# A two-layer diffusion trunk on one core: the output projection split in two stages, scores over all 128 rows, and a searched order

## The chip, the core and the metric

The kernel runs on one core of a Trainium2 chip. A core has five engines that run side by side, each with its own list of instructions, in order: TensorE (PE) multiplies matrices and transposes, VectorE (DVE) and ScalarE (ACT) work on tiles element by element, GpSimd (POOL) does small side jobs, and SyncE (SP) issues transfers (DMA). They wait for each other through semaphores. The metric is the time of one execution on the device in microseconds (us).

## The reference

Two layers run over 256 latent tokens (a grid of 4 x 64) and 128 context tokens, width 1024. Cut to what matters:

```python
def layer(x, mod, lp):
    h = rms(x, g_mix) * (1 + mod[1]) + mod[0]
    cq, ckv, krope, na_q, na_k, na_v, df_q, df_k, df_v = split(h @ w_in)
    o_mla = softmax_attend(...)         # 6 heads of width 64, keys of 96
    o_na  = neighbourhood_attend(...)   # 6 heads of 64; latent keys get a learned bias or -1e30
    o_df  = diff_attend(...)            # 4 heads: softmax(s1) - lam * softmax(s2), then RMSNorm
    mix = concat([o_mla, o_na, o_df]) @ w_out         # 384 + 384 + 256 rows of w_out
    x = x + mod[2] * mix
    h = rms(x, g_ffn) * (1 + mod[4]) + mod[3]
    return x + mod[5] * ((silu(h @ w_gate) * (h @ w_up)) @ w_down)
```

Context tokens attend to context tokens; latent tokens attend to cached context keys and their latent keys in one softmax. The keys and values of the context are outputs too.

## The kernel before

**Layout.** All 384 tokens stand side by side in the columns; the residual `xT` is [128, 8, 384], eight blocks of 128 features. Each projection runs as three products (`mm3`, L321 to L323): weights and data are split into a high half in a reduced format and the rest (`wh`, `wl`, made by ACT at L254 and DVE at L260), and hi x hi, lo x hi and hi x lo are summed. Raw weights come by SP into a ring of three `raw` tiles; `wh` and `wl` are rings of three slots each.

**Stages of a layer.** The input projection (`g1`, products `wh,hh`) is cut into six column chunks. The latent heads ("MLA") need chunk 0, the differential heads chunks 1 and 2, the three pairs of neighbourhood heads chunks 3 to 5. Attention works in steps made by `soft`: a score product (`score`, L1037), the maximum of a row on DVE (`maxima`, L1045), the exponential on ACT with its row sum (`exps`, L1056), the division on DVE (`norm`, L1061 and L1066), a transpose on PE (`turn`, L1004), a copy by ACT, and then the product with the values (`out`, L1139 and L1142). `pair` does this for two heads of MLA (`mla`) or of the neighbourhood group (`near`); `diff` does it for one differential head. The result of a pair is one block of 128 rows for the output projection: blocks 0 to 2 (`oxh`, `oxl`) are MLA, 3 to 5 neighbourhood and 6 and 7 differential (`o`).

**Neighbourhood scores before.** The queries of two heads stand in one tile, one head in rows 0 to 63 and the other in rows 64 to 127, and so do the keys; a head's score product takes its 64 rows. For a latent query tile, `bias` (L1100) adds a [128, 256] bias to the latent part of the score in the accumulator, and then `maxima` reads all 384 columns.

**Output projection.** For each of eight output blocks m, eight row blocks k of `w_out` are summed in one accumulator (order `ks`); `gated` (L534) then adds the result, times its gate, to `xT`. Blocks 0 to 2 (`OUT_EARLY`) are tasks of the plan below, block 3 only gets its weights split in the plan (`AHEAD`), and blocks 3 to 7 follow after it. After each block come its square (`norm_square`, L456), the running sum (L464) and the gained, split rows `fh`, `fl` (`gain_split`, L528 and L529) for the feed-forward, whose gate and up projections follow (products `fh,wh`), then the down projection.

**What sets the order.** From a layer's start to output block 2, every piece of work is a `Task` with an engine, a duration in us, a priority, its predecessors and the buffers it takes (`take`) or frees (`ROOM`: three `z`, two `s`, two `t` accumulators, three `raw`, three `w`, ...). `Plan.order` runs a greedy simulation on these durations and on the hops between engines (`HOPS`): each free engine takes the ready task of lowest priority number whose buffers are free. The instructions are then emitted in order of the tasks' planned starts, and each engine keeps that order. Dense work (`DENSE`) has high numbers and fills in. The durations are the planner's, not the chip's. Behind the plan, a scheduler of the compiler orders the engines' work.

## Time and profile before

| | |
|---|---|
| median of 3 runs (lowest to highest) | 1035.77 us (1035.76 to 1036.49) |
| profiled execution | 1036.13 us, span 1034.4 us |
| granted PE clock, mean | 0.986 |
| PE busy | 1012.3 us, 98%, 6074 matmuls |
| DVE, ACT, POOL busy | 719.5, 509.1 and 172.7 us |
| read from memory | 158.12 MB |

The span runs from the first to the last instruction. An engine is busy while one of its instructions runs. Matmuls overlap in the pipeline, so the time from one start to the next is what a matmul costs in a row of them, and a row's duration is longer. A type of f32 is written for both formats in PE's rows, and one product in full format shows as two matmuls. Layer 0 attends until about 215 us, layer 1 from about 545 to 717.

### The profile page before, as it was taken

The numbers are of one execution on the slowest core, as the hardware profiler recorded it, in microseconds if no ns is written. First come the engines' busy times: TensorE is split into PE (matmuls) and PEld (weight loads), VectorE is DVE, ScalarE is ACT, GpSimd is POOL, SyncE is SP. The second block draws the span as 40 slices with busy tenths as digits, with TensorE's granted clock in tenths as the row PEclk, the third lists the DMA queues.
The fourth block names the chain that finished last, engine by engine and source line by source line (L and its number), as shares of the span: only waits on it lengthen the run. The fifth ranks groups of instructions, "written<-read, shape, count | busy, mean of one in ns | idle before, by whom it ended". The sixth has DMA issues, their size and how long they took to land.

```text
span 1034.4 us, 16528 instructions
## 1 busy us (share of the span) xinstructions
PE 1012.3 (98%) x6074; PEld 933.0 (90%) x6074; DVE 719.5 (70%) x1599; ACT 509.1 (49%) x1180; POOL 172.7 (17%) x263
## 2 busy tenths in 40 slices
PE   8999999989999999999999999989999999999998
PEld 7877779679999999999978878867999999999998
DVE  5677787955999999963455887766869755554332
ACT  3466778745433333343326668766653334333221
POOL 2266223201001001100024533230010000000000
PEclk9999999989999999999999999969999999999999
DMA  9865444125575757684463232410376434343441
GB/s 356 331 202 190 161 153 138 58 82 202 165 243 185 233 177 232 206 273 131 123 226 101 81 125 71 154 54 9 123 249 199 125 120 137 108 123 111 139 137 42
DMA packets 129681, 162.25 MB, mean 157 GB/s; under 512 B 5056, under 2 KB 111680, under 8 KB 127296
## 3 DMA queue, kind: packets, MB, share of 16 engines
q1 hardware_dynamic: 121184, 132.76, 40.3%
q0 software_dynamic: 6832, 27.77, 7.7%
q8 instruction: 48, 0.79, 0.3%
q10 hardware_dynamic: 1584, 0.66, 0.2%
q14 instruction: 33, 0.27, 0.1%
HBM read 158.12 MB, written 3.05 MB: 156 GB/s over the span
## 4 chain that ended last, share of the span: by engine, by line
PE 76%; DVE 2%; ACT 1%; POOL 1%; issue 1%; ACTq 0%; DVEq 0%; POOLq 0%
PE z L321 11%; PE z L323 11%; PE z L322 11%; PE t L322 6%; PE t L321 6%; PE t L323 6%; PE s L322 5%; PE s L323 5%; PE s L321 5%; PE s L1037 2%; PE t L1004 2%; PE t L1139 1%; POOL small L542 1%; PE t L1376 1%; PE z L1037 1%
## 5 line engine op out<-in xcount | busy, mean ns | idle before, releaser
L254 ACT ACTIVATE wh<-raw 128x1024 fp32r<-128x1024 f32 (+2 forms) x216 | 201.5, 934 | 366.0 <-PE z L322 138.8
L260 DVE TENSOR_TENSOR wl<-raw,wh 128x1024 fp32r<-128x1024 f32 (+2 forms) x216 | 230.7, 1070 | 111.6 <-ACT wh L254 111.2
L321 PE MATMUL z<-fh,wh 128*128 128x386 f32 x304 | 103.2, 339 | 0.0
L322 PE MATMUL z<-fl,wh 128*128 128x386 f32 x304 | 103.0, 339 | 0.0
L323 PE MATMUL z<-fh,wl 128*128 128x386 f32 x304 | 102.6, 338 | 0.0
L444 DVE CUSTOM_DVE_ANT_0 sums<-wt,sums,pcol 128x1024 f32<-128x1024 f32 x80 | 102.2, 1278 | 0.3 <-DVE small L1578 0.3
L321 PE MATMUL z<-wh,hh 128*128 128x384 f32 (+1 forms) x264 | 99.9, 379 | 1.1 <-ACT hh L514 0.5
L323 PE MATMUL z<-wh,hl 128*128 128x384 f32 (+1 forms) x264 | 90.3, 342 | 0.5 <-DVE hl L522 0.5
L322 PE MATMUL z<-wl,hh 128*128 128x384 f32 (+1 forms) x264 | 89.8, 340 | 0.0
L542 POOL TENSOR_TENSOR small<-small,mhalf 128x4 f32<-128x4 f32 (+4 forms) x58 | 73.2, 1262 | 4.8
L321 PE MATMUL s<-fh,wh 128*128 128x386 f32 x200 | 68.2, 341 | 0.0
L321 PE MATMUL t<-fh,wh 128*128 128x386 f32 x200 | 68.1, 340 | 0.0
L322 PE MATMUL t<-fl,wh 128*128 128x386 f32 x200 | 67.8, 339 | 0.0
L322 PE MATMUL s<-fl,wh 128*128 128x386 f32 x200 | 67.8, 339 | 0.0
L323 PE MATMUL t<-fh,wl 128*128 128x386 f32 x200 | 67.5, 338 | 0.0
L323 PE MATMUL s<-fh,wl 128*128 128x386 f32 x200 | 67.5, 338 | 0.0
L438 POOL DMA_DIRECT2D wt<-in_w_modT x40 | 21.5, 539 | 273.7 <-DVE mod L444 190.8
L321 PEld LDWEIGHTS z<-wh,hh 128*128 128x128 f32 x264 | 49.8, 189 | 9.2 <-issue 4.2
L322 PEld LDWEIGHTS z<-fl,wh 128*128 128x128 f32 x304 | 57.5, 189 | 0.0
L323 PEld LDWEIGHTS z<-fh,wl 128*128 128x128 f32 x304 | 57.3, 188 | 0.0
L321 PEld LDWEIGHTS z<-fh,wh 128*128 128x128 f32 x304 | 57.2, 188 | 0.0
L1056 ACT ACTIVATE e<-s,small 128x384 f32<-128x384 f32 (+1 forms) x102 | 51.0, 506 | 12.2 <-DVE small L1045 11.2
(316 smaller groups left out, 2422.8 us busy)
## 6 DMA issues: line engine op xcount, KB each, us to landing
raw<-in_w_gate SPq DMA_DIRECT2D x22, 1024.0 KB, 6.0
raw<-in_w_up SPq DMA_DIRECT2D x22, 1024.0 KB, 5.4
raw<-in_w_down SPq DMA_DIRECT2D x32, 704.0 KB, 4.8
wt<-in_w_modT POOLq DMA_DIRECT2D x40, 512.0 KB, 4.3
raw<-in_w_mod SPq DMA_DIRECT2D x16, 1024.0 KB, 5.0
raw<-in_w_in SPq DMA_DIRECT2D x40, 384.0 KB, 3.9
raw<-in_w_out SPq DMA_DIRECT2D x8, 1024.0 KB, 5.5
qu<-in_w_mod SPq DMA_DIRECT2D x8, 512.0 KB, 7.4
```

The costliest lines, as they stand in the source:

```text
L254: nc.scalar.activation(hi, src, AF.Copy)
L260: nc.vector.tensor_tensor(lo, src, hi.bitcast(F32), op=ALU.subtract)
L321: nc.tensor.matmul(out, sh, mh, start=first, stop=False)
L322: nc.tensor.matmul(out, sh, ml, start=False, stop=False)
L323: nc.tensor.matmul(out, sl, mh, start=False, stop=last)
L438: nc.gpsimd.dma_start(self.w[:, self.loaded % 3], w_modT[l, c * P:(c + 1) * P])
L444: nc.vector.tensor_tensor_reduce(self.junk, self.w[:, self.n % 3], self.s[:, v], 1.0, pcol[l][:, PC_BMOD + c:PC_BMOD + c + 1], ALU.mult, A ...
L542: nc.gpsimd.tensor_tensor(out, t[:, :n], mhalf[:, :n], op=ALU.pow)
L1004: nc.tensor.transpose(pt[:, b, :], x, ident)
L1037: nc.tensor.matmul(ps[:, i, :], q, k, start=True, stop=True)
L1056: nc.scalar.activation(x["e"][i], ps[:, j, :], AF.Exp, bias=x["mx"][:, i:i + 1], accum_out=x["su"][:, i:i + 1])
L1139: nc.tensor.matmul(po[64 * i:64 * i + 64, 0:NL], vv[:, b, v0 + i, :], p["pT"][i][:, b, :], start=(b == 0), stop=(b == 2), tile_position=(0 ...
```

## The change

1. *Two stages.* The first three row blocks of the output projection (the MLA heads) become tasks of their own for all eight output blocks: three `mm3` into a `z` accumulator, and a `gated` that adds them to `xT` at once (`part`). Their weights come in two transfers of [3, 512] and four splits of [3, 256]. The second stage sums the other five row blocks; its weights are [5, 256] a transfer and [5, 128] a split, and it adds to `xT` with a second `gated`.

2. *Full-row scores.* Each neighbourhood head gets a query tile of 128 rows with zeros in the other head's half; `naq` becomes a two-column scale with a zero half in each column, and ACT writes the queries twice. The tiles are four (`nu[0]`), used in turn by six heads, so the transposes of the last pair wait for the scores of the first (`na_last`). The keys stay shared. The bias table is [128, 5, 128] with zeros for the context keys, and one `tensor_tensor_reduce` adds it, negates, writes the row back and takes the negated maximum; `exps` then scales by -1. The context scores of two heads share one accumulator.

3. *Order.* Some durations and hops of the planner change. `Plan.best` runs `order` up to 300 more times, each time with the priorities of 1 to 40 drawn tasks changed, and keeps the plan with the earliest planned end.

```diff
-HOPS = {('pe', 'act'): 0.2, ('pe', 'dve'): 0.16, ('act', 'pe'): 0.22, ('dve', 'pe'): 0.27, ('pool', 'dve'): 0.06, ('act', 'dve'): 0.15, ('dve', 'act'): 0.15}
+HOPS = {('pe', 'act'): 0.22, ('pe', 'dve'): 0.22, ('act', 'pe'): 0.22, ('dve', 'pe'): 0.27, ('pool', 'dve'): 0.18, ('dve', 'pool'): 0.18, ('act', 'dve'): 0.15, ('dve', 'act'): 0.13}
...
+    def best(self):
...
+        for _ in range(ORDERS):
+            p = list(best)
+            for i in draw.sample(free, draw.choice((1, 2, 4, 8, 16, 40))):
+                p[i] = base[i] + draw.gauss(0, STIR if draw.random() < 0.8 else 5 * STIR)
+            try:
+                run(p)
+            except AssertionError:
+                continue
+            if self.end <= end:
+                end, best = self.end, p
+        return run(best)
...
+            for q in range(4):
+                w_order.append((("lat", l, q), ("lat", l, q // 2), w_out[l, 0:3 * P, q // 2 * 512:(q // 2 + 1) * 512].rearrange("(k p) c -> p k c", p=P), [3, 512],
+                                slice(0, 3), slice(q % 2 * 256, (q % 2 + 1) * 256), (3, 256)))
...
             def maxima():
+                x["mx"], i = small(n), 0
                 if bias:
-                    bias(x["b"][0][0])
-                x["mx"], i = small(n), 0
+
+                    s = x["b"][0][0][:, 0, :]
+                    s = s.rearrange("p (b k) -> p b k", k=P)
+                    nc.vector.tensor_tensor_reduce(s, s, bias(), -1.0, 3e38, ALU.add, ALU.min, x["mx"])
+                    return
...
-                    nc.scalar.activation(nu[0][:, j, t * P:(t + 1) * P], x["pt"][:, 0], AF.Copy, scale=naq)
+                    for i in range(2):
+                        nc.scalar.activation(nu[0][(2 * j + i) % 4][:, t * P:(t + 1) * P], x["pt"][:, 0], AF.Copy, scale=naq[:, i:i + 1])
...
-        ks = [0, 1, 2, 6, 7, 3, 4, 5]
+        ks = [6, 7, 3, 4, 5]
...
+        for q in range(4):
+            hi, lo, w, lead = weights(("lat", l, q), lead if q % 2 else None)
+            for m in (2 * q, 2 * q + 1):
+                x, prev = {}, None
+                for k in range(3):
...
+                        mm3(x["po"][:, :NT], w["h"][:, k, ms], w["l"][:, k, ms], *o_hl[k], k == 0, k == 2)
+                    prev = add(PE, 0.53, unit, after=[lo, prev, o_ready[k]], take=("z",) if k == 0 else (), frees=[hi], prio=DENSE + 1)
...
+                part.append(add(DVE, 0.82, lambda m=m, x=x: gated(l, m, x["po"], 16), after=[prev, gates], frees=[room], prio=DENSE / 2))
...
-        work = plan.order()
+        work = plan.best()
```

**Where rows move.** A row names line, operation, output <- inputs (with buffer numbers) and shape. First PE near the end of attention in layer 1. Before, from the transposes of the last neighbourhood pair (`tok`) on:

```order
L1209 MATMUL t_7823<-ident,tok_7736 128x128 x2
L1037 MATMUL z_7835<-ku_7112,qu_7111 128x384
L1004 MATMUL t_7843<-ident,e_7789 128x128 x3
L1209 MATMUL t_7859<-ident,tok_7763 128x128 x2
L1037 MATMUL z_7862<-ku_7112,qu_7111 128x384
L1376 MATMUL t_7870<-vd_6337,pd_7864 128x64 x3
L1004 MATMUL t_7880<-ident,e_7818 128x128 x3
L1004 MATMUL t_7893<-ident,dn_7288 128x128 x3
L1335 MATMUL t_7904<-identr,tok_7838 128x128 x4
L1376 MATMUL z_7930<-vd_6337,pd_7891 128x64 x3
L1335 MATMUL t_7942<-identr,tok_7847 128x128 x4
L1335 MATMUL t_7947<-identr,tok_7900 128x128 x4
```

Now, the stretch ahead of the last value product (`z_8314` and `z_8348` collect the latent row blocks, `dn` is a differential head):

```order
L1045 MATMUL t_8298<-ident,e_8259 128x128 x3
L1045 MATMUL t_8305<-ident,e_8266 128x128 x3
L357 MATMUL z_8314<-oxh_5911,wh_8058 128x384
L358 MATMUL z_8314<-oxl_5912,wh_8058 128x384
L359 MATMUL z_8314<-oxh_5911,wl_8078 128x384
L1045 MATMUL t_8322<-ident,e_8286 128x128 x3
L357 MATMUL z_8314<-oxh_5911,wh_8058 128x384
L358 MATMUL z_8314<-oxl_5912,wh_8058 128x384
L359 MATMUL z_8314<-oxh_5911,wl_8078 128x384
L1045 MATMUL t_8335<-ident,e_8295 128x128 x3
L357 MATMUL z_8314<-oxh_5911,wh_8058 128x384
```

Before, 37 rows in a line there (from the first score of that kind in a `z` accumulator to the first `oxh` row) belong to no projection; now transposes and latent row blocks take turns, and 54 of the layer's 72 latent row-block products come before the last value product.

Second, DVE in layer 0 just after the last neighbourhood pair. Before, from the first residual update (`xT`) on:

```order
L534 SCALAR_TENSOR_TENSOR xT<-z_2741,mod_101,xT 128x256
L534 SCALAR_TENSOR_TENSOR xT<-z_2741,mod_101,xT 128x128
L534 SCALAR_TENSOR_TENSOR xT<-z_2791,mod_101,xT 128x256
L534 SCALAR_TENSOR_TENSOR xT<-z_2791,mod_101,xT 128x128
L534 SCALAR_TENSOR_TENSOR xT<-z_2986,mod_101,xT 128x256
L534 SCALAR_TENSOR_TENSOR xT<-z_2986,mod_101,xT 128x128
L529 SCALAR_TENSOR_TENSOR fl_3058<-xT,aff_103,fh_3057 128x256
L529 SCALAR_TENSOR_TENSOR fl_3058<-xT,aff_103,fh_3057 128x128
L529 SCALAR_TENSOR_TENSOR fl_3058<-xT,aff_103,fh_3057 128x256
L464 TENSOR_TENSOR sq_3039<-sq_3039,sq_3043 128x384
L260 TENSOR_TENSOR wl_3048<-raw_2342,wh_3030 128x1024
L260 TENSOR_TENSOR wl_3076<-raw_3072,wh_3074 128x1024
```

Now, from the remainder of that pair's output (`o`) on:

```order
L1196 TENSOR_TENSOR o_2775<-t_3035,o_2774 128x384
L1619 TENSOR_TENSOR fl_3141<-mod_101,fh_3140 128x8x2
L570 SCALAR_TENSOR_TENSOR xT<-z_3050,mod_101,xT 128x256
L570 SCALAR_TENSOR_TENSOR xT<-z_3050,mod_101,xT 128x128
L291 TENSOR_TENSOR wl_3079<-raw_2686,wh_3072 128x640
L565 SCALAR_TENSOR_TENSOR fl_3141<-xT,aff_103,fh_3140 128x256
L570 SCALAR_TENSOR_TENSOR xT<-z_3068,mod_101,xT 128x256
L570 SCALAR_TENSOR_TENSOR xT<-z_3068,mod_101,xT 128x128
L565 SCALAR_TENSOR_TENSOR fl_3141<-xT,aff_103,fh_3140 128x128
L291 TENSOR_TENSOR wl_3098<-raw_2861,wh_3090 128x640
L570 SCALAR_TENSOR_TENSOR xT<-z_3094,mod_101,xT 128x256
L570 SCALAR_TENSOR_TENSOR xT<-z_3094,mod_101,xT 128x128
```

Before, three blocks' updates stand in a line ahead of the next splits (`wl`); now an update and a split of 640 columns take turns.

Third, SP in layer 0. Before:

```order
L1092 DMA bias_2042<-in_bias 128x384
L1092 DMA bias_2102<-in_bias 128x384
L244 DMA raw_2134<-in_w_out 128x8x256
L1190 DMA vn_2188<-in_cache 128x256
L1302 DMA tok_2279<-in_dfk 32x256 x4
L244 DMA raw_2342<-in_w_out 128x8x256
L244 DMA raw_3072<-in_w_out 128x8x256
L1204 DMA out_newc<-brief_2350 128x128
L244 DMA raw_3116<-in_w_out 128x8x256
L1204 DMA out_newc<-brief_2644 128x128
L1092 DMA bias_2774<-in_bias 128x384
L1092 DMA bias_2833<-in_bias 128x384
```

Now:

```order
L1137 DMA bias_2229<-in_bias 128x640
L1236 DMA vn_2278<-in_cache 128x256
L275 DMA raw_2292<-in_w_out 128x3x512
L1250 DMA out_newc<-brief_2454 128x128
L275 DMA raw_2500<-in_w_out 128x3x512
L1137 DMA bias_2547<-in_bias 128x640
L1137 DMA bias_2601<-in_bias 128x640
L275 DMA raw_2686<-in_w_out 128x5x256
L1250 DMA out_newc<-brief_2825 128x128
L275 DMA raw_2861<-in_w_out 128x5x256
L275 DMA raw_3155<-in_w_out 128x5x256
L275 DMA raw_3190<-in_w_out 128x5x256
```

The loads of `w_out` were four in a layer and are six, the first two for the latent rows; the last two bias tables moved from behind the last `w_out` load to ahead of the third.

## The prediction

> **What bounds the kernel now.** The page comes first: who is busy, and the clock by slices.

> ```profile
> span 1034.4 us, 16528 instructions
> ...
> PE 1012.3 (98%) x6074; PEld 933.0 (90%) x6074; DVE 719.5 (70%) x1599; ACT 509.1 (49%) x1180; POOL 172.7 (17%) x263
> ...
> PEclk9999999989999999999999999969999999999999
> ```

> TensorE (PE) is busy 98% of the span, so only PE's time counts. Two of the forty clock digits are below 9: the ninth slice and, far lower, the 27th. Next come busy times by stretch; "x" counts instructions, PEclk is the granted clock.

> ```profile
> core 0: us, PE busy (x) PEld busy (x) DVE busy (x) ACT busy (x) POOL busy (x), PEclk, DMA share, GB/s
> ...
> 50.00:215.00 165.00, 162.19 (x1034) 127.13 (x1034) 127.24 (x357) 120.91 (x384) 61.06 (x90) 1.00 0.45 144
> 215.00:230.00 15.00, 11.33 (x50) 10.12 (x49) 9.36 (x21) 6.92 (x13) 0.00 (x0) 0.77 0.38 120
> 230.00:525.00 295.00, 295.00 (x1680) 293.65 (x1679) 229.85 (x427) 114.13 (x173) 21.17 (x39) 1.00 0.61 197
> ...
> 545.00:675.00 130.00, 126.16 (x749) 109.33 (x750) 99.81 (x262) 93.83 (x285) 52.80 (x76) 1.00 0.33 105
> 675.00:700.00 25.00, 22.38 (x87) 14.31 (x87) 16.77 (x48) 15.34 (x54) 9.08 (x16) 0.59 0.17 53
> 700.00:725.00 25.00, 24.52 (x156) 19.24 (x155) 17.01 (x50) 16.31 (x53) 1.11 (x2) 1.00 0.01 1
> ```

> From 230 to 525 (layer 0's last output blocks and its feed-forward) PE never idles at full clock: 1680 matmuls in 295 us, 0.176 us each, and nothing to win. What a stretch loses is its idle time (length less busy) and its clock loss (length times 1 - PEclk):
> - 215:230, the output projection of layer 0: 3.67 idle + 0.23 x 15 = 3.45, so 7.1 us.
> - 675:700, the end of attention in layer 1: 2.62 + 0.41 x 25 = 10.25, so 12.9 us.
> - 50:215, 545:675 and 700:725: idle 2.81, 3.84 and 0.48, so 7.1 us.

> PE's timeline shows why. Columns: start, duration, engine, line, names, rows x columns, moving shape, count, idle before. First layer 1:

> ```profile
> 673.99 0.34 PE L323 MATMUL z<-wh,hl 128*128 128x384 f32 x1
> ...
> 677.07 0.76 PE L1037 MATMUL s<-ku,qu 64*128 64x128 f32 x4
> 678.62 0.66 PE L1209 MATMUL t<-ident,tok 128*128 128x128 f32 x2 [0.79 <-ACT e L1056]
> 679.21 1.65 PE L1037 MATMUL z<-ku,qu 64*128 64x384 f32 x2
> ...
> 690.03 1.95 PE L1335 MATMUL t<-identr,tok 128*128 128x128 f32 x8
> ```

> The last input projection ran at 673.99; after it only links of the softmax chains are left. The same score pair that takes 0.91 us warm (656.04 below) takes 1.65 at 679.21: half clock. The idle before 678.62 is only 0.79 us, so thin work alone cooled it. Now layer 0:

> ```profile
> 217.78 0.44 PE L321 MATMUL z<-oxh,wh 128*128 128x384 f32 x1
> ...
> 218.73 0.45 PE L321 MATMUL s<-oxh,wh 128*128 128x384 f32 x1 [0.32 <-ACT wh L254]
> ...
> 220.08 0.45 PE L321 MATMUL z<-oxh,wh 128*128 128x384 f32 x1 [0.72 <-ACT wh L254]
> 220.36 0.34 PE L322 MATMUL z<-oxl,wh 128*128 128x384 f32 x1
> 223.32 0.69 PE L323 MATMUL z<-oxh,wl 128*128 128x384 f32 x1 [2.62 <-DVE wl L260]
> ```
> ```profile
> 216.85 2.04 DVE L534 SCALAR_TENSOR_TENSOR xT<-z,mod,xT 128x256 f32<-128x256 f32 x6 [1.66 <-PE z L323]
> ...
> 222.05 3.49 DVE L260 TENSOR_TENSOR wl<-raw,wh 128x1024 fp32r<-128x1024 f32 x3
> ...
> 229.47 0.74 DVE L534 SCALAR_TENSOR_TENSOR xT<-z,mod,xT 128x256 f32<-128x256 f32 x2 [2.54 <-PE z L323]
> 230.44 1.23 DVE L260 TENSOR_TENSOR wl<-raw,wh 128x1024 fp32r<-128x1024 f32 x1 [0.22 <-ACT wh L254]
> 231.58 0.74 DVE L529 SCALAR_TENSOR_TENSOR fl<-xT,aff,fh 128x256 fp32r<-128x256 f32 x2
> 232.24 0.55 DVE L464 TENSOR_TENSOR sq<-sq,sq 128x384 f32<-128x384 f32 x1
> ```

> PE waits 0.32, 0.72 and 2.62 us for weight halves of the later output blocks. The three early blocks end together, since each holds one of three weight slots until its last row block arrives; the next weights are split only then, and on VectorE (DVE) behind six residual updates (2.04 us). The gap costs the clock too (0.77 above).

> **The change part by part.**

> (a) *Full-row scores.* In the neighbourhood group, 24 score products (3 pairs, 2 heads, 2 query tiles, 2 layers) go from 64 rows to 128, with zeros in the other head's half. Scores of this type have 64 or 96 rows in the trace; each first row below is followed by PE's next work.

> ```profile
> 108.92 0.81 PE L1037 MATMUL s<-ku,qu 96*128 96x384 f32 x2
> 109.57 0.49 PE L1004 MATMUL t<-ident,e 128*128 128x128 f32 x3
> ```
> ```profile
> 656.04 0.91 PE L1037 MATMUL s<-ku,qu 64*128 64x384 f32 x2
> 656.88 0.44 PE L1209 MATMUL t<-ident,tok 128*128 128x128 f32 x2
> ```
> ```profile
> 147.02 1.55 PE L1037 MATMUL s<-ku,qu 64*128 64x384 f32 x4
> 148.51 0.45 PE L321 MATMUL z<-wh,hh 128*128 128x384 f32 x1
> ```

> 96 rows take 0.65 us from start to next start, 64 rows 0.84. I take 0.65 for 128 rows, being no half of the array: 20 warm scores x -0.19 = -3.8 us (four lie in the cold stretch, counted in (b)). Ends: two 64-row scores of different halves side by side took 1.49 together, 0.745 each, so 24 x -0.095 = -2.3; the other end 24 x -0.19 = -4.6. [...]

> (b) *End of attention, layer 1.* The eight output blocks' first three row blocks (72 matmuls a layer) now need only latent heads, and input projection is spread further: in the new order its last 12 matmuls stand beside the last pair's transposes, and 54 of the 72 follow before the last value product; before, 37 rows there held no projection at all. 54 x 0.176 = 9.5 us of dense work, moved, not added. If it keeps the clock, up to 12.9 us go. The last pair's chain (four scores, maxima, exponentials, transposes) stays and waits somewhere: I keep 1.5 us. A latent block also holds one of three z banks until its residual update; a late one stops PE's next block and all behind it, which rival 4 prices. Take -11.4; ends 0 and -12.9.

> (c) *Output projection, layer 0.* After the last value product the blocks run one after another, 15 matmuls (2.63 us) each, and slots come free one by one, so a split has two blocks' time. Take -6.6 of 7.1; ends 0 and -7.1. Late next is (e).

> (d) *The other stalls, 7.1 us.* The searched order changes everywhere, from a planner whose durations are raised towards the measured. Some stalls go, others come: half, -3.5; ends +3.5 and -7.1.

> (e) *VectorE in the output stage.* Residual update 0.74, second half of the gained rows 0.74, sum 0.55 (rows above) and the split of 640 columns:

> ```profile
> L444 DVE CUSTOM_DVE_ANT_0 sums<-wt,sums,pcol 128x1024 f32<-128x1024 f32 x80 | 102.2, 1278 | 0.3 <-DVE small L1578 0.3
> ...
> L1045 DVE TENSOR_REDUCE small<-s 128x1 f32<-128x384 f32 x67 | 35.7, 552 | 4.6 <-PE s L1037 3.7
> L260 DVE TENSOR_TENSOR wl<-raw,wh 128x640 fp32r<-128x640 f32 x32 | 26.4, 825 | 52.0 <-ACT wh L254 52.0
> ...
> L1100 DVE TENSOR_TENSOR s<-s,bias 128x256 f32<-128x256 f32 x17 | 7.2, 426 | 1.4 <-PE s L1037 1.2
> ...
> L444 DVE DVE_READ_ACCUMULATOR2_ANT mod<- 128x1 f32 x80 | 6.6, 82 | 0.0
> ```

> That is 2.86 us per block against PE's 2.63; before it was 3.26 against 24 x 0.176 = 4.2. Five blocks a layer: 5 x 0.23 = 1.2 us late at the feed-forward, twice: +2 (ends 0 and +5, if the two gate splits of 1.23 queue as well).

> (f) *VectorE and ScalarE in attention.* Sixteen more residual updates: 16 x 0.74 = +11.8 us. Bias add (0.426) and maximum (0.552) of 24 scores, 23.5 us, become one custom operation reading PSUM, which the trace does not show at 384 columns. By the 1024-column one of 1.278 scaled, 0.48 + 0.08 read-out; unscaled, 1.36. I take 0.65, nearest the maximum over the same 384: 15.6. Net +4 us on VectorE, beside PE while the windows below hold; 0 on the path, up to +13 at 1.36 (rival 4).

> ```profile
> 175.00:200.00 25.00, 23.81 (x150) 18.79 (x149) 22.35 (x64) 20.15 (x66) 7.01 (x11) 1.00 0.21 64
> ```
> ```profile
> L1212 ACT ACTIVATE qu<-t,naq 128x128 f32<-128x128 f32 x17 | 6.0, 367 | 3.8 <-PE t L1209 2.8 <-ACT vn L1193 0.4 <-DVE ku L1215 0.4
> ```

> Queries are written twice: 18 x 0.367 = 6.6 us more on ScalarE, which has 4.85 of 25 us free there even in the fullest stretch: 0.

> (g) *Queues.* SP issues six w_out loads a layer instead of four, same bytes, and larger bias tables (320 KB for 192). The last two bias tables now wait in SP's queue for a table to come free, ahead of the third w_out load of layer 0 and the fourth of layer 1; the gate weights stand behind those.

> ```profile
> DMA to landing us min/median/max: 2.2/3.1/10.3
> ```

> At a median 3.1 us (5.2 scaled by size) and tens of us ahead, 0; ends 0 and +2. POOL gains nothing.

> (h) *Added wait.* Six heads share four query buffers, so the last pair's transposes on PE wait for the first pair's scores; the order has both pairs' scores well ahead. Behind them stand projection rows: 0, at most the last link of (b).

> Sum: -3.8 - 11.4 - 6.6 - 3.5 + 2 = -23.3 us. The profiled execution took 1036.13 us (span 1034.4 and 1.7 around it), 0.4 above the median of 1035.77; 1036.1 - 23.3 = 1012.8.

> **The rivals.**

> 1. *Layer 1 stays cold.* The 54 products may be too thin between transposes. For it: the clock fell behind an idle of 0.79 us. Against: before there was no projection row at all. (b) gives 0 and (d) 2.5: 1036.1 - 3.8 - 6.6 - 2.5 + 2 = 1025.2. [...]

> 2. *Every stall goes.* -3.8 - 12.9 - 7.1 - 7.1 = -30.9, so 1005.2. For it: idle that moves behind filler vanishes. Against: the last chain, and (e).

> 3. *The order does nothing on the chip.* The search minimizes its own plan, whose durations are no trace; stalls would return elsewhere, about 1035. Against: (a) and (c) hang on no fine timing.

> 4. *Slower: the custom operation binds VectorE.* Place: neighbourhood scores, 175 to 215 and 650 to 700. VectorE has 2.65 of 25 us free, 4.2 in 40, 8.5 in two layers; its extra is 11.8 + 24 (x - 0.978). From x = 0.83 us it overflows. At 1.36 it is 21 us, 12.5 beyond the room: PE waits for maxima, (a), (b) and (d) fall away, 1036.1 - 6.6 + 12.5 + 2 = 1044. Slower than before from an overflow of 4.6 us, x = 1.03. For it: the only such row is 1.278; against: it has 1024 columns.

> **How the numbers follow.** My forecast (1006 to 1020) 0.62; rival 1 0.18; rival 2 0.08; rival 3 0.05; rival 4 0.07. Predicted: 1012.8. The range 1003 to 1027 takes in the forecast and rivals 1 and 2 with a margin for gaps the windows count as busy; it leaves out rivals 3 and 4, 0.12. A measurement tells 0.2% (2.1 us) from no change. Faster 0.62 + 0.18 + 0.08 and 0.01 of rival 3 = 0.89; same 0.03; slower 0.07 + 0.01 = 0.08.

> **What would show it.** (a): 128-row scores with 0.65 us to the next start. (b): clock 1.00 in every 25 us stretch of layer 1. (c): no wait above 1 us for weight halves after the last value product of layer 0. (d): idle outside these stretches near 3.5 us. (e): PE idle or repeated waits for fh, fl where the feed-forward begins, 1 us a layer. (f): the custom operation near 0.65 us. It is wrong if one clock digit stays near 6 in layer 1's attention, if VectorE passes 23 of 25 us there, or if the start to 50 us, which I leave as it is, grows.

## The result and the profile after

The changed kernel took 1010.96 us (median of 4 runs, 1010.33 to 1011.29) beside 1036.13 of the kernel before on the same chip: ratio 0.9753, 95% interval 0.9736 to 0.977, 25.2 us faster. The prediction was 1012.8, within 1003 to 1027. The profiled execution took 1011.29. One execution further down, the profiled one of experiment 6 (1649 us), ran at a granted clock of 0.555 over its whole span and serves no comparison. The page of the changed kernel, span, busy times and clock by slices:

```profile
span 1009.5 us, 16623 instructions
...
PE 995.5 (99%) x6074; PEld 929.6 (92%) x6074; DVE 721.8 (71%) x1637; ACT 512.6 (51%) x1206; POOL 174.4 (17%) x263
...
PEclk9999999999999999999999999999999999999999
```

No digit of the clock below 9 is left. The same stretches as before (columns as there; they are fixed in time, and from layer 0's feed-forward on the changed kernel's work stands 10 us or more earlier in them):

```profile
50.00:215.00 165.00, 162.18 (x1051) 131.06 (x1044) 129.94 (x370) 122.73 (x391) 61.59 (x90) 1.00 0.45 145
215.00:230.00 15.00, 15.00 (x87) 15.00 (x87) 12.98 (x31) 10.33 (x21) 0.00 (x0) 1.00 0.60 185
230.00:525.00 295.00, 294.01 (x1688) 289.14 (x1690) 228.93 (x431) 112.92 (x169) 24.08 (x42) 1.00 0.63 202
525.00:545.00 20.00, 18.00 (x84) 14.87 (x77) 13.11 (x29) 9.73 (x30) 11.16 (x18) 0.91 0.34 125
545.00:675.00 130.00, 129.01 (x798) 112.02 (x797) 105.68 (x288) 100.99 (x320) 56.09 (x79) 1.00 0.33 105
675.00:700.00 25.00, 23.63 (x155) 19.66 (x155) 22.29 (x67) 19.50 (x61) 5.37 (x7) 1.00 0.21 64
700.00:725.00 25.00, 25.00 (x146) 24.81 (x143) 20.99 (x47) 15.33 (x32) 0.00 (x0) 1.00 0.49 154
```

The output stage of layer 0 (215:230) has neither idle time nor clock loss, where 7.1 us stood. The end of attention in layer 1 (675:700) lost 12.9 us and now loses 1.37, all of it idle. Idle in 545:675 fell from 3.84 to 0.99; in 50:215 it did not move (2.81, now 2.82). Between 230 and 545 more is lost than before: idle 2.99 us against 1.65, in part because work that stood after 545 has moved in, and one piece of 3.41 us at half clock at 536.0. Before, the last of these stretches was:

```profile
525.00:545.00 20.00, 18.35 (x113) 13.17 (x111) 12.58 (x25) 6.65 (x11) 9.60 (x14) 1.00 0.69 228
```

The attention of layer 1, which before goes on to 723.1, now ends at 700.1. PE's timeline of 676 to 680 shows what stands there:

```profile
676.51 0.60 PE L1078 MATMUL s<-ku,qu 128*128 128x384 f32 x2
676.95 0.34 PE L357 MATMUL z<-oxh,wh 128*128 128x384 f32 x1
...
678.36 0.34 PE L359 MATMUL z<-oxh,wl 128*128 128x384 f32 x1
679.28 0.41 PE L1255 MATMUL t<-ident,tok 128*128 128x128 f32 x2 [0.58 <-DVE tok L1270]
679.44 0.42 PE L357 MATMUL z<-oxh,wh 128*128 128x384 f32 x1
```

Latent row blocks (`oxh,wh`) stand on both sides of the wait for `tok`, where before only transposes and scores stood. At the start, the first input product moved back from 21.05 to 22.87 us, behind products of the modulation, one of which waits for a transfer. Up to there PE has done 128 matmuls of the modulation instead of 96 and was idle for 2.13 us instead of 2.40, so the delay is work done earlier and not a loss:

```profile
21.87 0.30 PE L408 MATMUL m<-ku,sv 128*32 128x128 f32 x2 [0.87 <-DMA ku<-in_w_mod]
...
22.87 0.46 PE L357 MATMUL z<-wh,hh 128*128 128x416 f32 x1
```

The custom operation in the trace's list of one line's instructions (shortest, median and longest ns):

```profile
L1087 DVE DVE_READ_ACCUMULATOR2_ANT small<- x24: 83/141/144, 138.5 to 692.1; 128x1 f32 x24
...
L1087 DVE CUSTOM_DVE_ANT_0 s<-s,bias x11: 555/566/600, 139.6 to 690.5; 128x384 f32<-128x384 f32 x11
```

0.57 us and 0.14 for reading the accumulator out: 0.70 where 0.65 was taken.

Two tables compare all kernels. Both are worked out from one profiled execution each; those of S and R ran above their medians (1036.9 and 1034.9 us). In the first, idle is the span less PE's busy time, clock loss is half of the time that the trace's clock record holds at half clock (the piece at the very end of a span left out), and the rest is busy time less clock loss, in us (an estimate: not all work took twice as long at half clock, as the score row of 679.21 in the prediction, 1.65 us beside 0.91 at 656.04):

| kernel | median | against before | span | idle | clock loss | rest |
|---|---|---|---|---|---|---|
| before | 1036.1 | | 1034.4 | 22.1 | 13.7 | 998.7 |
| S: two stages | 1033.0 | -3.5 | 1035.1 | 19.6 | 17.1 | 998.4 |
| R: full-row scores | 1032.1 | -4.4 | 1033.1 | 24.9 | 13.7 | 994.5 |
| C: new planner costs | 1026.0 | -10.6 | 1024.5 | 20.3 | 3.4 | 1000.8 |
| O: costs and search | 1020.8 | -15.7 | 1019.4 | 18.7 | 1.7 | 999.0 |
| S + O | 1022.6 | -14.1 | 1020.7 | 18.2 | 5.1 | 997.4 |
| R + O | 1013.0 | -23.7 | 1011.9 | 16.4 | 1.7 | 993.8 |
| S + R + C | 1020.4 | -16.1 | 1018.2 | 19.7 | 5.1 | 993.4 |
| S + R + O (the change) | 1011.0 | -25.2 | 1009.5 | 14.0 | 1.7 | 993.8 |
| the change, other seed | 1012.2 | -23.9 | 1010.8 | 13.8 | 3.4 | 993.6 |

"Against before" is against the median of before on the same chip (1036.1 to 1036.7); differences between two other kernels are taken from their medians, and by the column they come out up to 0.5 us smaller where the two ran on different chips. From before to the change: idle -8.1, clock -12.0, rest -4.9. The second table has the lengths of the stages, from the first and last product of each in PE's rows (attention until the last value product, output until the first feed-forward product; the feed-forward stages are alike to 0.3 us except in one kernel, told below; the layers' boundary takes 8.1 to 9.8):

| kernel | start | attention 0 | output 0 | attention 1 | output 1 |
|---|---|---|---|---|---|
| before | 21.1 | 192.7 | 31.7 | 187.3 | 26.2 |
| S | 20.9 | 195.6 | 30.3 | 187.9 | 24.0 |
| R | 21.1 | 199.4 | 26.7 | 180.3 | 28.7 |
| C | 22.7 | 190.8 | 29.9 | 179.1 | 26.7 |
| O | 22.7 | 188.3 | 26.7 | 177.5 | 27.2 |
| R + O | 22.6 | 188.6 | 27.8 | 170.2 | 27.2 |
| the change | 22.9 | 189.5 | 23.0 | 174.3 | 24.6 |

### The profile page after: what moved, and what is told of

Same layout as the page of the kernel before. It is cut to its first block, busy times and chain, and to the rows that moved or that the text cites. A ratio compares the mean times of both kernels' runs of the same rounds, so it can differ in the third digit from the quotient of the medians.

```text
span 1009.5 us, 16623 instructions
## 1 busy us (share of the span) xinstructions
PE 995.5 (99%) x6074; PEld 929.6 (92%) x6074; DVE 721.8 (71%) x1637; ACT 512.6 (51%) x1206; POOL 174.4 (17%) x263
## 4 chain that ended last, share of the span: by engine, by line
PE 89%; ACT 5%; DVE 2%; POOL 1%; DMA 1%; issue 1%; ACTq 0%; DVEq 0%; POOLq 0%
PE z L357 13%; PE z L359 13%; PE z L358 13%; PE t L358 6%; PE t L357 6%; PE t L359 6%; PE s L357 5%; PE s L358 5%; PE s L359 5%; PE s L1078 4%; PE t L1045 2%; PE m L408 2%; PE t L1181 1%; PE s L952 1%; PE s L750 1%
## 5 line engine op out<-in xcount | busy, mean ns | idle before, releaser
L285 ACT ACTIVATE wh<-raw 128x768 fp32r<-128x768 f32 (+3 forms) x224 | 203.5, 909 | 365.4 <-PE z L358 138.1
L291 DVE TENSOR_TENSOR wl<-raw,wh 128x768 fp32r<-128x768 f32 (+3 forms) x224 | 231.8, 1035 | 112.5 <-ACT wh L285 110.9
L480 DVE CUSTOM_DVE_ANT_0 sums<-wt,sums,pcol 128x1024 f32<-128x1024 f32 x80 | 102.3, 1278 | 0.3 <-ACT sums L469 0.3
L578 POOL TENSOR_TENSOR small<-small,mhalf 128x4 f32<-128x4 f32 (+4 forms) x58 | 75.5, 1302 | 4.8
L1101 ACT ACTIVATE e<-s,small 128x384 f32<-128x384 f32 (+1 forms) x114 | 57.8, 513 | 15.2 <-DVE small L1090 9.0
```

The lines of the kernel that those rows point to most:

```text
L285: nc.scalar.activation(hi, src, AF.Copy)
L291: nc.vector.tensor_tensor(lo, src, hi.bitcast(F32), op=ALU.subtract)
L480: nc.vector.tensor_tensor_reduce(self.junk, self.w[:, self.n % 3], self.s[:, v], 1.0, pcol[l][:, PC_BMOD + c:PC_BMOD + c + 1], ALU.mult, A ...
L578: nc.gpsimd.tensor_tensor(out, t[:, :n], mhalf[:, :n], op=ALU.pow)
L1101: nc.scalar.activation(x["e"][i], ps[:, j, :], AF.Exp, bias=x["mx"][:, i:i + 1], scale=-1.0 if bias else 1.0, accum_out=x["su"][:, i:i + 1])
```

## The experiments

**1. One part at a time.** The change has three parts that can be built alone. The two stages alone are the hunks on `part`, `("lat", ...)` and `ks` of the diff above:

```diff
-        ks = [0, 1, 2, 6, 7, 3, 4, 5]
+        ks = [6, 7, 3, 4, 5]
...
+                part.append(add(DVE, 0.82, lambda m=m, x=x: gated(l, m, x["po"], 16), after=[prev, gates], frees=[room], prio=DENSE / 2))
```

> The kernel before with the two-stage output projection alone (64-row scores, old planner costs, no search). Theory (the split carries the end of layer 1 and the output stage of layer 0): terms (b) and (c) with (e), -11.4 - 6.6 + 2 = -16 us, so about 1020; clock 1.00 in layer 1's last 25 us of attention and no wait over 1 us for weight halves after the last value product of layer 0. Rival (the split needs the searched order to fall into the gaps): less than half of that, 1028 or more, with a cold stretch left in layer 1.

Measured: 1032.96 us, ratio 0.9962 (0.9949 to 0.9974). The rival's condition holds: the cold stretch is still there, and layer 1's attention is as long as before.

```profile
675.00:700.00 25.00, 22.88 (x92) 16.13 (x92) 18.15 (x52) 16.88 (x61) 9.26 (x17) 0.61 0.06 16
```

In its timeline of PE, the first latent row block comes at 697.35 us. VectorE's timeline has the splits for the first three of the four sets of latent weights, the first done by 670.2 and the third by 680.1 (rows of 669.19 and 679.11):

```profile
677.69 0.33 PE L1042 MATMUL s<-ku,qu 128*128 128x128 f32 x2
679.25 0.44 PE L1214 MATMUL t<-ident,tok 128*128 128x128 f32 x2 [1.23 <-DVE tok L1228]
...
697.35 0.67 PE L326 MATMUL z<-oxh,wh 128*128 128x384 f32 x1
```
```profile
669.19 0.96 DVE L260 TENSOR_TENSOR wl<-raw,wh 128x768 fp32r<-128x768 f32 x1 [1.04 <-ACT wh L254]
...
679.11 0.95 DVE L260 TENSOR_TENSOR wl<-raw,wh 128x768 fp32r<-128x768 f32 x1
```

The weights were there in time; the old order puts the rows behind the cold stretch, not into it. What in the plan holds them back there was not looked into. The wait of 2.62 us for weight halves is gone, but two stretches of 6.8 us at half clock stand in layer 0's attention instead (185.6 and 199.3).

The full-row scores alone (hunks on `naq`, `nu`, `bias` and `maxima`):

```diff
-                    nc.scalar.activation(nu[0][:, j, t * P:(t + 1) * P], x["pt"][:, 0], AF.Copy, scale=naq)
+                    for i in range(2):
+                        nc.scalar.activation(nu[0][(2 * j + i) % 4][:, t * P:(t + 1) * P], x["pt"][:, 0], AF.Copy, scale=naq[:, i:i + 1])
```

> The kernel before with the full-row scores and their custom operation alone. Theory (a 64-row score costs 0.84 us to the next start, a 128-row one 0.65): -3.8 us, between -2.3 and -4.6, so about 1032; the cold stretch and the 2.62 us wait for weights stay. Rival A (the scores sit in stretches that wait for the softmax chains anyway): within 2 us of before. [...]

Measured: 1032.05, ratio 0.9955 (0.9938 to 0.9972): the theory's size, though its runs spread from 1027.95 to 1034.9. Its rest fell by 4.2, its idle grew by 2.8. What was to stay did not: PE has no wait for weight halves in layer 0's output stage, and half clock moved from two places to five, none over 10.2 us.

The planner's costs and the search alone (hunks on `HOPS`, on durations and on `best`):

```diff
-        work = plan.order()
+        work = plan.best()
```

> The kernel before with the new planner costs and the search alone. Theory (term (d)): -3.5 us, between -7 and +3.5; the cold stretch of layer 1 (clock 0.59) stays, since nothing dense is left to put there, so 1029 to 1040. Rival (the search is what carries the whole change): 1020 or less. Rival (planned durations tell nothing of the chip): within 2 us of before.

Measured: 1020.77, ratio 0.984 (0.9825 to 0.9854): just above the bound of the first rival, far from the theory. The cold stretch of layer 1 is gone without the two stages:

```profile
675.00:700.00 25.00, 22.14 (x133) 14.16 (x131) 22.16 (x65) 19.03 (x61) 6.92 (x11) 1.00 0.19 61
```

PE is idle there for 2.86 us, more than the 2.62 of before, and holds the clock. What differs is where projection rows stand. The input products of layer 1 are spread over 146.0 us (138.1 before), and after the last of them 11.9 us pass until the next projection row, a latent row (`oxh`) of the three early blocks at 687.54; before it was 26.3 us, in S 20.4. This length alone does not decide: in R it is 30.9, with 10.2 us of half clock around it. The clock record shows more than the idle time: in all kernels here the half clock comes in pieces of 3.41 us or a multiple (6.83 and 20.48 in before, which are two and six, and 3.41 in the changed kernel). Cutting before's rows on its own edges gives (length; PE busy; clock is the third number from the end):

```profile
592.98:596.39 3.41, 2.06 (x15) 1.77 (x15) 2.76 (x6) 2.06 (x6) 1.72 (x3) 1.00 1.01 379
674.90:678.31 3.41, 2.27 (x15) 1.66 (x14) 2.53 (x7) 2.99 (x12) 2.93 (x5) 1.00 0.76 258
678.31:681.73 3.42, 3.11 (x9) 1.72 (x9) 3.19 (x11) 2.28 (x12) 2.82 (x5) 0.50 0.02 5
...
685.14:688.55 3.41, 2.41 (x11) 1.69 (x9) 2.04 (x5) 2.77 (x11) 0.87 (x2) 0.50 0.20 58
...
695.38:698.79 3.41, 3.41 (x14) 1.93 (x15) 1.36 (x5) 1.66 (x5) 0.91 (x2) 0.50 0.00 0
698.79:702.21 3.42, 3.42 (x27) 3.00 (x24) 2.56 (x7) 2.46 (x7) 0.42 (x1) 1.00 0.21 58
```

After a window with 2.27 us of PE busy, six follow at half clock. PE's busy time alone does not settle after which window: 592.98 has less of it (2.06 us) than 674.90 and no half clock followed. Cutting the traces of all kernels here but that of experiment 6 in this way, from 50 us on, gives: all nine windows at full clock with under 1.9 us of PE busy were followed by half clock and none with over 2.62 was; of those between, 14 were and 47 were not.

**2. Costs or search.** O without the search, and the change without it; the edit in both:

```diff
-        work = plan.best()
+        work = plan.order()
```

> The kernel before with the new planner costs alone, in the plan's first order (no search). With the search it took 1020.8, -15.7 us, most of it clock. The planner's own ends are 210.40 and 176.60 us here, 208.41 and 175.48 with the search. Theory (the costs themselves, nearer to the measured, keep dense work back for the end): 1020 to 1026. Rival (it is the search that spreads the dense work): 1032 or more, with the cold stretches near 680 and in layer 0 still there.

> The changed kernel with the plan's first order instead of the searched one (two stages, full-row scores and new planner costs stay). The planner's own ends are 222.75 and 185.98 us against 216.16 and 181.67 with the search, 10.9 us later. Theory (the search carries term (d) and some of the late end of layer 1): 3 to 6 us slower than the changed kernel, 1014 to 1017. Rival A (the plan's ends hold on the chip): 10.9 slower, about 1022. Rival B (the searched order is noise on the chip): within 2 us, 1009 to 1013.

Measured: 1026.0 (0.9901, 0.9886 to 0.9915) for the costs alone, at the far end of the theory's range; 1020.35 (0.9837, 0.982 to 0.9853) for the change without search. The costs alone bring 10.6 us, and their clock loss is 3.4 where before's is 13.7. The search adds 5.2 on top of the costs and 9.4 within the change, where the planner had promised 3.1 and 10.9: the gain within the change is nearer to rival A's than to the theory's 3 to 6, and on the costs alone more than promised.

**3. Parts taken out of the change.** Without the full-row scores (S + O), and without the two stages (R + O); each edit takes back one part's hunks.

> The changed kernel without the full-row scores (two stages, new costs, search). Theory (64-row scores cost PE 4.3 us more, as the kernel with full-row scores alone showed, and in a searched order little of it hides in idle time): 1013 to 1016. Rival A (the saved time turns into waits, as in that kernel, which gained 4.4 in its median but 3 us of idle time in its profile): within 2 us of the changed kernel, 1009 to 1013. Rival B (bias add and maximum apart load VectorE more): over 1018.

> The changed kernel without the two stages (full-row scores, new costs, search; OUT_EARLY stays 3). Theory (with a searched order the split still gives 5 to 7 us: it fills waits, and three early blocks no longer hold the weight slots): 1016 to 1018. Rival A (the order alone does what the split was credited with): within 2 us of the changed kernel. Rival B (terms (b) and (c) of the prediction are the split's own): 1024 or more, with a cold stretch in layer 1.

Measured: 1022.56 (0.9864, 0.985 to 0.9879) without the full-row scores, 11.6 slower than the change; 1012.97 (0.977, 0.9754 to 0.9786) without the two stages, 2.0 slower. The theory falls in both: rival B's number (over 1018) holds for the first, rival A (within 2 us) for the second. Between S + O and the change lie 3.6 us of rest, 3.4 of clock loss and 4.2 of idle (first table): the scores' PE time is a third of what they are worth there. R + O has no cold stretch in layer 1 and the shortest attention of all (170.2). The two stages shorten the output stages (by 4.8 and 2.6) and lengthen attention by what they move there (0.9 and 4.1): a move of work, with 2 us of gain.

**4. How much is the draw of an order.** The search with another seed:

```diff
-        draw = random.Random(0)
+        draw = random.Random(1)
```

> The changed kernel with another seed of the search (planned ends 215.51 and 181.29 us against 216.16 and 181.67: 1.0 us earlier). It measures how far the time hangs on which order the search happens to find. Theory (orders of like planned end differ by 1 to 3 us on the chip, so a marginal of 2 us, as that of the two stages, tells nothing, and one of 11.6, as that of the full-row scores, is partly luck): 1008 to 1014. Rival (planned ends hold): 1009.5 to 1010.5.

Measured: 1012.17 (0.9767, 0.9752 to 0.9782), 1.2 slower though planned 1.0 shorter. So the 2.0 of the two stages cannot be told from the luck of an order. The 11.6 is more than the largest difference between drawn orders seen here (5.4, next), but S + O was drawn only once.

More orders, and layer 0's start left in its place:

```diff
-ORDERS, STIR = 300, 3.0
+ORDERS, STIR, HOLD = 1500, 3.0, 19.0
...
+        if not self.warm:
+            free = [i for i in free if tasks[i].start > HOLD]
```

> The changed kernel with 1500 searched orders instead of 300, and in layer 0 only tasks planned to start after 19 us may be redrawn, so that the start keeps its order (planned ends 215.77 and 181.15). Theory (the changed kernel lost 1.8 us at the start, where the first input products moved behind a PE row that waits for a transfer, and the plan does not see it): first input product back near 21 us, 1008 to 1010, faster than the changed kernel by 1 to 2.5. Rival (noise between orders is larger): anywhere from 1008 to 1014.

Measured: 1016.32 (0.9804, 0.9789 to 0.982), 5.4 slower than the change; both expectations missed. The theory's loss at the start was none, as the result shows: PE only did other work first. The start did come back (first input product at 20.98), but layer 0's attention and output took 3.9 us more, and its gate and up projections 4.8 more, which no order of the plan touches. PE's and then ScalarE's timeline there:

```profile
253.76 0.45 PE L359 MATMUL z<-fh,wh 128*128 128x386 f32 x1 [2.12 <-ACT wh L287]
```
```profile
239.92 0.51 ACT L494 ACTIVATE sq<-xT 128x384 f32<-128x384 f32 x1
249.56 1.28 ACT L471 ACT_TABLE_LOAD   x1 [9.13 <-DMA sums<-in_crow]
...
252.67 2.93 ACT L287 ACTIVATE wh<-raw 128x1024 fp32r<-128x1024 f32 x3
```

The activation of `sums` and its table load stand ahead of three weight halves in ScalarE's list and wait 9.13 us for a transfer; PE then waits 2.12 us for a half, and a window at half clock follows at 256.1. The changed kernel's ScalarE at that place waits for nothing at this row:

```profile
245.82 1.28 ACT L469 ACT_TABLE_LOAD   x1
247.12 1.92 ACT L469 ACTIVATE sums<-sums 128x2048 f32<-128x2048 f32 x1
```

What made that transfer late was not tested; the DMA engines are as busy from 240 to 250 in both (0.94 here, 0.97 in the changed kernel).

**5. Three early blocks.** The prediction's cause for the stall in layer 0's output stage:

```diff
-OUT_EARLY = 3
+OUT_EARLY = 1
```

> The kernel before with one output block in the plan instead of three (OUT_EARLY = 1; blocks 1 to 7 follow one after another). Theory (three early blocks, each holding one of three weight slots until the last row block, cause the 2.62 us wait and the cold windows of layer 0's output stage): that stage's loss of 7.1 us falls by 5 to 7, and 2 blocks of dense work less before the end of attention cost layer 1 nothing that is not already cold: 1029 to 1031. Rival (those blocks' products are needed as filler in the attention's end): the stall goes, but attention ends later by as much, 1034 to 1040.

Measured: 1037.86, ratio 1.0016 (0.9998 to 1.0035): the rival's number. The output stage of layer 0 fell from 31.7 to 25.5 us and the 2.62 us wait is gone, but attention before it took 5.0 us more. Part of this is a move: 63 output products stand ahead of the last value product where 51 did (2.1 us at 0.176). From its first input product to the feed-forward, layer 0 is 1.2 us shorter (223.2 against 224.4). What is lost is in layer 1: in the profiled execution, the longest of its runs at 1043.96, 34.1 us of half clock stood there (before: 20.5 there, 27.3 in all). So without the three blocks the wait is gone; they alone do not make it, since R keeps them in the old order and has none. That their products are missed as filler, the rival's reason, is not shown: in layer 1, 42 output products stand ahead of the last value product where 45 did.

**6. Useless work.** Lowest-priority tasks for layer 1 in the kernel before, 18 with three products each:

```diff
+            def filler():
...
+                    nc.tensor.matmul(fill["pm"][:, :NT], identr, o_hl[0][0], start=True, stop=True)
+            for _ in range(18):
+                add(PE, 0.53, filler, after=[o_ready[0]] + list(dense), prio=DENSE + 9)
```

> The kernel before with 54 useless 128x128 by 128x384 products (9.5 us of PE work at 0.176, into an accumulator nobody reads) as lowest-priority tasks of layer 1, free to run once the last input projection is placed; layer 0 is as before. Theory (the clock follows how full PE is in a window of 3.41 us, whatever the work): the 20.5 us at half clock near 680 shrink to 7 or less, so 6 to 10 us less for at most 3 us of filler that stands in the way: 1029 to 1033, and 9.5 us of added work make the kernel faster. Rival A (the stretch is bound by the softmax chain, not by the clock): 1034 to 1037 with the clock at 1.00. Rival B (the filler delays the chain): slower, 1040 or more.

Measured: 1031.8 us (1031.31 to 1032.09 without the profiled execution), ratio 0.9955 (0.9938 to 0.9971): 9.5 us of products that nobody reads make the kernel 4.3 us faster, in the theory's range and outside both rivals'. The granted clock of these four runs is 0.997, beside 0.986 to 0.988 for before on the same chip: by it some 11 us less are lost to the clock (an estimate, 0.014 of 1034 against 0.003 of 1030). So the clock is where the gain comes from; that it comes from the stretch near 680 is argued, since the only trace is of the execution named in the result.

**7. The price of a score.** Two stages and full-row scores in the old order, with seven series of products at the end:

```diff
+        for i in range(20):
+            h = slice(64 * (i % 2), 64 * (i % 2) + 64)
+            nc.tensor.matmul(pb[3 + i % 2][:, :NT], ident[h, :], xT[h, 1, :], start=True, stop=True)
...
+        for i in range(12):
+            nc.tensor.matmul(pb[0][:, :NT], ident[0:64, :], xT[0:64, 4, :], start=True, stop=True)
+            for j in range(3):
+                nc.tensor.transpose(pb[1][:, j * P:(j + 1) * P], xT[:, 5, j * P:(j + 1) * P], ident)
```

> Two stages and full-row scores with the old planner costs and no search, and behind its end seven series of useless products in full format on PE (20 each of 64 rows in one half, 64 rows in alternating halves, 96 rows, 128 rows; 12 each of a 64-row or 128-row product followed by three transposes); the series add some 70 us. On the order: theory (two stages and full-row scores add up without the new order): the kernel's own part ends near 1028, half clock left in layer 0 and 1; rival (the two together fill the gaps): near 1020, as with the new costs. On the price of a score: theory (half an array is slower): 0.84 us a product with 64 rows, 0.65 with 96 and 128, the alternating halves 0.7 to 0.75. [...] Rival B (64 rows cost the same in a series, and the 0.84 comes from the change to what follows): all series 0.65 or less, and 64 rows with transposes 0.15 to 0.2 us longer a round than 128 rows.

The order: the kernel's own last product ends at 1022.87 us, which with the changed kernel's 3.7 from there to the end of the span is 1026.5, or 1028.2 with the 1.7 around it: the theory, S and R add up and no more (-3.5 - 4.4). It is one execution, and R's own runs spread over 7 us. The price, PE's timeline: 64 rows of one half in a line; 64 rows in alternating halves; then rounds of a product and three transposes, 64 rows first, 128 rows after:

```profile
1062.89 0.81 PE L1675 MATMUL s<-xT,ident 64*128 64x384 f32 x2
1063.54 0.81 PE L1675 MATMUL t<-xT,ident 64*128 64x384 f32 x2
...
1074.29 6.82 PE L1678 MATMUL z<-xT,ident 64*128 64x384 f32 x39
1081.05 0.91 PE L1680 MATMUL s<-xT,ident 96*128 96x384 f32 x2
...
1121.05 0.55 PE L1686 MATMUL t<-ident,xT 128*128 128x128 f32 x3
1121.53 0.91 PE L1684 MATMUL s<-xT,ident 64*128 64x384 f32 x2
1122.37 0.55 PE L1686 MATMUL t<-ident,xT 128*128 128x128 f32 x3
1122.75 0.81 PE L1688 MATMUL s<-xT,ident 128*128 128x384 f32 x2
1123.40 0.49 PE L1690 MATMUL t<-ident,xT 128*128 128x128 f32 x3
1123.72 0.81 PE L1688 MATMUL s<-xT,ident 128*128 128x384 f32 x2
```

In a line, 64 rows cost 0.65 us to the next start (1062.89 to 1063.54), and so do the series of 96 and of 128 rows. In alternating halves 39 matmuls take 6.76 us (1074.29 to 1081.05), 0.35 a product of two, about half of 0.65: they overlap. With transposes a round is 0.48 + 0.84 = 1.32 us with 64 rows (from 1121.05) and 0.65 + 0.32 = 0.97 with 128 (from 1122.75). So a 64-row product is not dear, the change between it and a full-row one is, by 0.35 us there and back. (The 96-row score in the prediction's row of 108.92 took 0.65 on its way to full rows.) The theory falls and rival B holds: none of the four series without transposes takes more than 0.65 a product; of the round's difference it had half.

## Why the prediction came out right, and where it was wrong

The total is right to 2 us; the causes behind it mostly are not, so the closeness is in good part luck. By its own steps:

- **(a) full-row scores, -3.8.** The rest column says -4.2 (R), -5.2 (R + O against O) and -3.6 (the change against S + O), so the size of PE's saving stands, and two 128-row scores of the changed kernel take 1.29 us to the next start, 0.65 each (687.21 below). The step that failed is the reason, "no half of the array" at 0.84 against 0.65: a 64-row product costs 0.65 too. The 0.84 was the way from 64 to 128 rows, and the way back, 0.16 a round, was left out; so were the 12 context scores that changed as well. The prediction took the row of 1.49 us for two halves side by side. That row is two scores one after the other: its four matmuls start 0.43, 0.32 and 0.32 us apart, and 1.49 is 0.65 + 0.84. The one pair of before whose matmuls start closer together takes 1.19 (200.83 below), and in the series of alternating halves a product takes 0.35 (experiment 7). Before, then changed:

```profile
200.83 1.26 PE L1037 MATMUL s<-ku,qu 64*128 64x384 f32 x4
202.02 0.44 PE L1004 MATMUL t<-ident,e 128*128 128x128 f32 x2
```
```profile
687.21 1.45 PE L1078 MATMUL s<-ku,qu 128*128 128x384 f32 x4
688.50 0.49 PE L1045 MATMUL t<-ident,e 128*128 128x128 f32 x3
```

  That padding still saves PE time fits what the trace of before holds: 16 of the 24 scores stand alone among full-row work, as the rows of 656.04 and 656.88 in the prediction, six in pairs one after the other, two side by side. Their worth in time, 4.4 alone and 11.6 within the change, was missed: S + O has more idle and clock loss too. Which of their effects does that (one custom operation for two, VectorE 728.5 to 721.8 us busy, or context scores of two heads in one accumulator), or whether the one order drawn for S + O does, was not taken apart.
- **(b) end of attention in layer 1, -11.4.** The stretch went from 12.9 to 1.4 lost, -11.5: the size was right. The step that failed is the credit, "If it keeps the clock" put on the 54 latent row blocks. In the old order they do not get into the stretch at all (S: clock 0.61), and the new costs and search keep it at 1.00 without the two stages (O).
- **(c) output stage of layer 0, -6.6.** All 7.1 us went. The cause named holds in part: without the three early blocks the wait of before is gone (experiment 5). The credit fails: with these blocks kept, PE has no wait for weight halves there in R, C, O or R + O either. And a stall taken away there need not shorten the kernel: in experiment 5 layer 0 gained 1.2 us by it and the kernel nothing.
- **(d) other stalls, -3.5.** The idle of the three stretches named fell by 3.3, some of it moved ahead of 545. What failed is the reach given to the order: it was let move only these, and in (b) and (c) it carried nearly everything.
- **(e) VectorE late at the feed-forward, +2.** It did not come: PE has no idle time where either feed-forward begins (235.4 and 724.7), as these stretches of the changed kernel show:

```profile
225.00:240.00 15.00, 15.00 (x88) 15.00 (x87) 13.81 (x31) 10.50 (x20) 2.28 (x4) 1.00 0.63 208
240.00:250.00 10.00, 10.00 (x63) 10.00 (x63) 4.17 (x9) 5.78 (x5) 1.79 (x1) 1.00 0.97 345
700.00:740.00 40.00, 40.00 (x235) 39.81 (x232) 28.59 (x64) 23.66 (x40) 4.04 (x5) 1.00 0.64 213
```

  The 2 us that did not come nearly cancel what no term had: 1.3 us more idle time between 230 and 545 and 1.7 of clock at 536.0, less 0.9 us of idle time saved before 50. That is luck.
- **(f), (g), (h).** 0.70 for 0.65, far from the 0.83 (redone, 0.84) from which rival 4 binds VectorE; no wait on a queue, and none for the shared query buffers that shows.

Rival 3, "the order does nothing on the chip", was given 0.05, and its reason is the furthest off: new costs and search carry 15.7 alone, 17.2 on top of S and R (1028.2 to 1011.0). Rival 1's condition (the stretch stays cold) is what S alone does. Rival 2 asked too much: 14.0 us of idle time and 1.7 of clock stay.

## What to carry to other kernels

When PE is 98% busy and short of its clock, first find the windows in which it thins out, and ask which order of the work already there fills them; a restructuring that only supplies more filler does not help such a window until the order puts it there (S alone: clock 0.61 in the cold stretch, 0.59 before). A right total proves no term of the sum: build each part alone and each part left out, since the parts here are worth 3.5, 4.4 and 15.7 alone and 2.0, 11.6 and 17.2 within the change. And take a second draw of any searched order before believing a gain of 2 us, as an order planned shorter came out 5.4 us slower, 4.8 of it in a projection that waited behind one late transfer. Time at a stage's start is no loss where PE did other work in it: compare idle time, not the moment at which a stage begins.
